# The start of a two-block transformer kernel: order of the first loads, squares summed on TensorE, low parts made between value tiles, constant products ahead of the real ones

## The chip, the cores and the metric

The kernel runs on one core of one Trainium2 chip. The metric is the device time of one execution in microseconds, as the median of several runs. TensorE (PE) does the matrix products, VectorE (DVE) and ScalarE (ACT) work on the elements, GpSimd (POOL) does a power function here, and SyncE (SP) issues most DMAs. ACT and POOL can issue DMAs too.

## What is computed

The reference is a stack of two parts in float32: two layers of a four-branch mixer (differential attention, gated linear attention, latent attention, windowed attention) with a convolutional feed-forward, and then two layers with gated feed-forwards and other mixers. The change touches only the first step of the first layer, which is an RMS norm of 272 tokens (16 meta tokens and 256 inputs) of width 1024, and the product of the normed tokens with the wide matrix `w_in`:

```python
h = jnp.concatenate([meta, x], axis=1)          # 272 tokens x 1024
for l in range(DEPTH):
    u = _rms_norm(h, norm_mix_pre[l])           # x * rsqrt(mean(x*x) + eps) * gain
    (a_q, a_k, a_v, ...) = jnp.split(u @ w_in[l], offsets, axis=-1)
    ...                                         # four branches, gates, w_out
    h = h + _rms_norm(merged @ w_out[l], norm_mix_post[l])
    ...                                         # feed-forward
...                                             # the second block, final norm
```

## The kernel before, in words

The tokens stand transposed in SBUF: `h` holds 8 tiles (k = 0 to 7) of 128 channels by 272 tokens. Every big product is done as three passes in a reduced float32 format: a high part and a low part of both operands, high times high, high times low and low times high (`mm3`). So each weight tile of 128 output columns (8 x 128 values on each partition) is split: `split` writes the high part `wh` on ACT (L114), `split_low` writes the low part `wl` on DVE as the difference (L122). The normed tokens are split in the same way into `uh` and `ul`. Three buffers hold split weight tiles, and three hold raw chunks of 1 MB with two tiles each (`raw`, loaded by `pump_dma`, L100). Products on plain float32 operands run as two instructions each.

Work of each engine runs in the order in which the program writes it; there is no planner behind it. The start goes like this. `setup` issues four token loads (L424, two k each) on SP, then two small loads on ACT, the first three raw chunks on SP, and fourteen small loads on SP (L457: tables, vectors, sinks, constants). Successive DMAs share a limited set of completion semaphores, so an issue can wait for an earlier load to land. `pre` then squares the tokens on ACT as they land (L762), adds the squares of all four pairs on DVE (L764, L766), sums over channels on PE against a column of ones (`tok_sums`, three token blocks), makes mean plus epsilon on DVE (L269), the power -1/2 on POOL (L271), and spreads the three short columns over 128 partitions on PE (`spread`). Ahead of the power in the program, `prefetch(2)` splits the high parts of the first two weight tiles, and behind it `advance` makes their low parts on DVE.

`normed` is the loop that follows: for each k it writes gain times token times spread value (L302, DVE, named `w` in the trace), its high part `uh` (L304, ACT), and, one k later, the low part `ul` (L295, DVE). The first product (`first_gemm` with a group of two weight tiles) goes over k and issues six matmuls for each, three for each of the two tiles; its third and sixth need `wl` of the first and of the second weight tile. Behind the pair come single tiles of 24 matmuls each. The third weight tile's high part is written on ACT behind the last `uh`, its low part on DVE behind the last `ul`.

`gps` and `aps` hand out PSUM buffers in turn, four of each.

Of the kernel before, what the change touches and what calls it, by code (L numbers as in the profile page):

```python
# [13 lines left out]
MUL, ADD, SUB, MAX, MIN = ALU.mult, ALU.add, ALU.subtract, ALU.max, ALU.min  # L14
# [5 lines left out]
KD = 8  # L20
T = 272
META = 16
SEQ = 256
# [11 lines left out]
NR = 3  # L35
# [27 lines left out]
class Kern:  # L63
# [25 lines left out]
        self.phase = -1  # L89
        self.held = False  # L90

    def pump_dma(self):
        while self.n_free < len(self.chunks) and self.chunks[self.n_free].left == 0:
            self.n_free += 1
        while self.n_dma < min(self.n_free + NR, len(self.chunks)):
            c = self.chunks[self.n_dma]
            t = self.wp.tile([128, 2048], F32, tag="raw", name="raw", bufs=NR)
            n = c.nk * c.nc
            src = self.a["weights"][self.offset : self.offset + 128 * n]
            self.nc.sync.dma_start(out=t[:, :n], in_=src.rearrange("(p n) -> p n", p=128))  # L100
            self.offset += 128 * n
            c.tile = t[:, :n].rearrange("p (k c) -> p k c", k=c.nk)
            self.n_dma += 1
# [180 lines left out]
    def w1(self, n=T, bufs=4):  # L284
        return self.wk.tile([128, T], F32, tag="w1", name="w1", bufs=bufs)[:, :n]

    def normed(self, x, pr, gain, shift, n, dst):

        nc = self.nc
        uh, ul = dst  # L290

        def low(k, t):
            h = uh[:, k, :].bitcast(F32)
            if shift is None:
                nc.vector.tensor_tensor(out=ul[:, k, :], in0=t, in1=h, op=SUB)  # L295
            else:
                nc.vector.scalar_tensor_tensor(out=ul[:, k, :], in0=t, scalar=shift(k), in1=h, op0=ADD, op1=SUB)

        prev = None
        for k in range(KD):  # L300
            t = self.w1(n)
            nc.vector.scalar_tensor_tensor(out=t, in0=x[:, k, :], scalar=gain(k), in1=pr, op0=MUL, op1=MUL)  # L302
            if shift is None:
                nc.scalar.activation(uh[:, k, :], t, AF.Copy)  # L304
            else:
                nc.scalar.activation(uh[:, k, :], t, AF.Identity, bias=shift(k))
            if prev is not None:
                low(*prev)
            prev = (k, t)
        low(*prev)  # L310

# [91 lines left out]
    def setup(self):  # L403
        nc, a = self.nc, self.a
        c = self.const
        self.ident = c.tile([128, 128], F32, name="ident")
        self.ones32 = c.tile([128, 32], F32, name="ones32")
        nc.vector.memset(self.ones32, 1.0)
        self.ones = self.ones32[:, 0:1]
        self.zero = c.tile([128, 1], F32, name="zero")  # L410
        nc.vector.memset(self.zero, 0.0)
        self.mhalf = c.tile([128, 16], F32, name="mhalf")
        nc.vector.memset(self.mhalf, -0.5)
        self.shh = c.tile([128, 3], F32, name="shh")


        nc.scalar.activation(self.shh, self.mhalf[:, 0:3], AF.Square)
        self.vec = c.tile([128, sum(n for _, n in VECS)], F32, name="vec")
        self.vecs, o = {}, 0
        for name, n in VECS:  # L420
            self.vecs[name] = o
            o += n
        for k in range(0, KD, 2):
            nc.sync.dma_start(out=self.h[:, k : k + 2, :], in_=a["tokens"][:, k : k + 2, :])  # L424
        n0 = VECS[0][1]
        nc.scalar.dma_start(out=self.ident, in_=a["k_ident"])
        nc.scalar.dma_start(out=self.vec[:, :n0], in_=a["vecs"][:, :n0])
        self.pump_dma()
        self.tabx = self.mx.tile([33, 24], F32, tag="s1", name="tabx", bufs=2)
        nc.vector.memset(self.tabx, NEG)  # L430
        self.hot = self.mx.tile([33, 2, PITCH], F32, tag="s4", name="hot", bufs=3)
        self.dl = self.mx.tile([128, 2, 4, 64], F32, tag="v4", name="dl", bufs=3)
        self.tri = c.tile([128, 2, 128], F32, name="tri")
        self.perm = c.tile([128, 128], F32, name="perm")
        self.cs = c.tile([128, 2, T], F32, name="cs")
        self.lam = c.tile([128, 2], F32, name="lam")
        self.sinks = c.tile([128, 2, 8], F32, name="sinks")
        self.sinkm = c.tile([128, 2, 2], F32, name="sinkm")
        self.mod = c.tile([128, 144], F32, name="mod")
        self.n_mod = 0  # L440
        self.cc = c.tile([128, 8], F32, name="cc")
        s, d = a["swa_sinks"], a["diff_lambda"]
        loads = [
            (self.hot, a["k_hot"]), (self.tabx[0:32, 0:16], a["rel_bias_table"]),
            (self.tabx[0:32, 16:24], a["rel_bias_table"][:, 8:16]), (self.vec[:, n0:], a["vecs"][:, n0:]),
            (self.dl, bass.AP(tensor=d.tensor, offset=d.offset, ap=[[0, 128], [256, 2], [64, 4], [1, 64]])),
            (self.sinks, bass.AP(tensor=s.tensor, offset=s.offset, ap=[[0, 128], [8, 2], [1, 8]])),
        ]
        for h in range(4):
            loads.append((  # L450
                self.sinkm[32 * h : 32 * h + 32],
                bass.AP(tensor=s.tensor, offset=s.offset + h, ap=[[0, 32], [8, 2], [4, 2]]),
            ))
        loads += [(self.cc, a["c_2"].rearrange("a (p k) -> p (a k)", k=8))]
        loads += [(self.tri, a["k_tri"]), (self.perm, a["k_perm"]), (self.cs, a["k_cs"])]
        for dst, src in loads:
            nc.sync.dma_start(out=dst, in_=src)  # L457

    def setup2(self):

# [277 lines left out]
    def mixing(self, l):  # L738
        nc, a = self.nc, self.a
        S = {}  # L740
        r0, rn = (0, T) if l == 0 else (14, T - 14)
        blocks = [BLK["M"], BLK["A"], BLK["B"]]
        W = self.w["w_in"][l]
        x = (self.uh, self.ul)
# [12 lines left out]
        def pre():  # L757
            if l == 0:
                sq = S["merged"]
                acc = sq[:, 0:2, :]  # L760
                for k in range(0, KD, 2):
                    nc.scalar.activation(sq[:, k : k + 2, :], self.h[:, k : k + 2, :], AF.Square)  # L762
                    if k:
                        nc.vector.tensor_tensor(out=acc, in0=acc, in1=sq[:, k : k + 2, :], op=ADD)  # L764
                self.prefetch(2)
                nc.vector.tensor_tensor(out=acc[:, 0, :], in0=acc[:, 0, :], in1=acc[:, 1, :], op=ADD)  # L766
                sums = self.tok_sums([acc[:, 0, :]], blocks)
                r = self.pow_rsqrt(sums, 3, D)
                for j, t in enumerate(sums):
                    nc.vector.tensor_copy(self.shh[:, j : j + 1], t)  # L770
                self.advance()
                pr = self.spread(r, blocks)
                self.normed(self.h, pr[:, :T], lambda k: self.v("norm_mix_pre", l * 8 + k), None, T, x)
            nc.sync.dma_start(out=self.hd[l], in_=self.h)

        self.add(pre)

        def to(name, i, w=128):
# [1642 lines left out]
```

## Time and profile before

| what | us |
|---|---|
| median of 3 runs | 2278.74 |
| lowest and highest of them | 2277.09, 2283.06 |
| the profiled execution's own time | 2284.18 |
| its span, first to last instruction | 2281.6 |
| TensorE busy in it | 2192.9 (96%) |
| VectorE busy | 1612.5 (71%) |
| ScalarE busy | 1217.2 (53%) |

The page gives shares over the whole span. The stage that the change touches is the first 25 us, so it is read from the timeline of each engine there: when an instruction starts, how long it takes, and in brackets how long its engine sat idle before it and who released it. The granted TensorE clock is read from the page's strip and from the views by stretch; ahead of the first record of the clock (at 21.6 us) these views show full speed, and the spacing of the matmuls has to tell the clock there.

### The profile page before, as it was taken

What the parts mean: (1) busy time and instruction counts of PE and PEld (TensorE: products, weight loads), DVE (VectorE), ACT (ScalarE), POOL (GpSimd) and SP (SyncE); (2) the same over time, 40 slices, a digit from 0 to 9 for tenths busy, and PEclk for the clock granted to TensorE, in tenths of its full rate; (3) what the DMA queues carried; (4) which work ended last, traced back from release to release, by engine and by line L of the source; (5) the groups of instructions that cost most, each with busy time, mean ns of one, the idle gap of its engine ahead of it and who ended that gap; (6) DMA issues with size and microseconds to landing.
All of it is one profiled execution on the core that took longest, in us unless ns stands there. A gap on an engine that the chain in (4) does not pass through costs nothing. (4 is left out here: it accounts for less than half of the span.)

```text
span 2281.6 us, 41972 instructions
## 1 busy us (share of the span) xinstructions
PE 2192.9 (96%) x17048; PEld 2070.0 (91%) x17048; DVE 1612.5 (71%) x2809; ACT 1217.2 (53%) x2221; POOL 240.6 (11%) x285
## 2 busy tenths in 40 slices
PE   7999999999999999999999899986999999999998
PEld 7888888899988798788999799986999999989998
DVE  5655454798885555547989887798877787778553
ACT  4555244577556544445775554465644554466442
POOL 0220111100031001112000100066100000001000
PEclk9999999999999999999999899997999999999999
DMA  7553233454764343324657687733687687744551
GB/s 271 190 183 114 100 102 114 172 206 170 278 242 158 112 148 107 112 97 172 227 184 289 260 302 273 255 111 111 229 283 277 241 303 272 268 174 140 206 177 70
DMA packets 73618, 439.21 MB, mean 192 GB/s; under 512 B 14285, under 2 KB 15629, under 8 KB 25936
## 3 DMA queue, kind: packets, MB, share of 16 engines
q1 hardware_dynamic: 62736, 419.66, 51.3%
q0 software_dynamic: 10400, 16.79, 2.5%
q8 instruction: 133, 2.18, 0.4%
q14 instruction: 61, 0.50, 0.1%
q10 hardware_dynamic: 288, 0.07, 0.0%
HBM read 433.12 MB, written 10.01 MB: 194 GB/s over the span
## 5 line engine op out<-in xcount | busy, mean ns | idle before, releaser
L227 PE MATMUL g<-uh,wh 128*128 128x256 f32 (+2 forms) x3560 | 1034.0, 290 | 18.9 <-ACT uh L322 6.2
L227 PE MATMUL g<-ul,wh 128*128 128x256 f32 (+2 forms) x3560 | 1025.1, 288 | 9.5 <-DVE ul L326 5.9
L227 PE MATMUL g<-uh,wl 128*128 128x256 f32 (+2 forms) x3560 | 1021.8, 287 | 2.7 <-DVE wl L122 2.7
L122 DVE TENSOR_TENSOR wl<-raw,wh 128x1024 fp32r<-128x1024 f32 (+2 forms) x660 | 785.8, 1196 | 274.2 <-ACT wh L114 273.7
L114 ACT ACTIVATE wh<-raw 128x1024 fp32r<-128x1024 f32 (+2 forms) x660 | 670.2, 1020 | 335.5 <-PE g L227 298.9
L227 PEld LDWEIGHTS g<-uh,wh 128*128 128x128 f32 x3560 | 680.1, 191 | 42.2 <-issue 13.5
L227 PEld LDWEIGHTS g<-ul,wh 128*128 128x128 f32 x3560 | 678.7, 191 | 14.0 <-DVE ul L326 6.9
L227 PEld LDWEIGHTS g<-uh,wl 128*128 128x128 f32 x3560 | 680.7, 191 | 3.7 <-DVE wl L122 3.4
L227 PE MATMUL g<-gh,wh 128*128 128x256 f32 (+1 forms) x1056 | 299.2, 283 | 0.0
L227 PE MATMUL g<-gh,wl 128*128 128x256 f32 (+1 forms) x1056 | 299.2, 283 | 0.0
L227 PE MATMUL g<-gl,wh 128*128 128x256 f32 (+1 forms) x1056 | 299.1, 283 | 0.0
L227 PEld LDWEIGHTS g<-gl,wh 128*128 128x128 f32 x1056 | 201.5, 191 | 0.0
L227 PEld LDWEIGHTS g<-gh,wh 128*128 128x128 f32 x1056 | 201.3, 191 | 0.0
L227 PEld LDWEIGHTS g<-gh,wl 128*128 128x128 f32 x1056 | 201.3, 191 | 0.0
L1717 DVE CUSTOM_DVE_ANT_0 adaw<-adaw,condb,vec 128x1024 f32<-128x1024 f32 x144 | 182.4, 1280 | 1.5 <-DMA adaw<-in_ada_t_dram 1.5
L1620 DVE SCALAR_TENSOR_TENSOR y<-edge,vec,y 128x272 f32<-128x272 f32 (+1 forms) x176 | 86.4, 493 | 28.5 <-ACT y L1615 25.4
L227 PE MATMUL g<-oh,wh 128*128 128x272 f32 (+1 forms) x296 | 87.9, 297 | 0.0
L227 PE MATMUL g<-ol,wh 128*128 128x272 f32 (+1 forms) x296 | 84.6, 286 | 0.0
L227 PE MATMUL g<-oh,wl 128*128 128x272 f32 (+1 forms) x296 | 84.5, 285 | 0.0
L1863 ACT ACTIVATE sg<-g 128x256 f32<-128x256 f32 x80 | 30.6, 382 | 99.9 <-PE g L227 99.8
L1224 ACT ACTIVATE gt<-g 128x272 f32<-128x272 f32 (+1 forms) x64 | 25.1, 392 | 107.7 <-PE g L227 107.7
L1252 POOL TENSOR_TENSOR merged<-merged,w 128x272 f32<-128x272 f32 (+1 forms) x48 | 37.9, 798 | 338.5 <-DVE w L1251 338.3
(377 smaller groups left out, 2434.2 us busy)
## 6 DMA issues: line engine op xcount, KB each, us to landing
raw<-in_weights_dram SPq DMA_DIRECT2D x294, 1024.0 KB, 4.9
adaw<-in_ada_t_dram SPq DMA_DIRECT2D x72, 1024.0 KB, 6.6
raw<-in_weights_dram SPq DMA_DIRECT2D x28, 768.0 KB, 4.8
skew<-scr POOLq DMA_DIRECT2D x6, 1086.0 KB, 22.7
h<-skew POOLq DMA_DIRECT2D x8, 544.0 KB, 4.4
h<-skew POOLq DMA_DIRECT2D x8, 512.0 KB, 5.4
condb<-cond SPq DMA_DIRECT2D x5, 512.0 KB, 4.7
hd<-h SPq DMA_DIRECT2D x2, 1088.0 KB, 9.1
```

The lines of the kernel that those rows point to most:

```text
L114: self.nc.scalar.activation(h3[:, :, d0 : d0 + n], c.tile[:, :, c0 : c0 + n], AF.Copy)
L122: self.nc.vector.tensor_tensor(out=l3[:, :, d0 : d0 + n], in0=c.tile[:, :, c0 : c0 + n], in1=h3[:, :, d0 : d0 + n].bitcast(F32), op=SUB,)
L227: self.nc.tensor.matmul(out, lhsT, rhs, start=start, stop=stop, skip_group_check=True)
L1224: nc.scalar.activation(t[:, :rn], ps[:, :rn], AF.Tanh, scale=0.5)
L1252: nc.gpsimd.tensor_tensor(out=mg, in0=mg, in1=t, op=ADD)
L1620: nc.vector.scalar_tensor_tensor(out=y, in0=e[:, o : o + on], scalar=cw(i), in1=y, op0=MUL, op1=ADD)
L1717: self.nc.vector.tensor_tensor_reduce(out=t[:, i, :], in0=t[:, i, :], in1=self.condb, scale=1.0, scalar=self.v("ada_b_2", c), op0=MUL, op1 ...
L1863: nc.scalar.activation(t, ps[:, :SEQ], AF.Silu)
```

## The change

In `setup`, the raw chunks are no longer issued, the two small loads on ACT change places, and the fourteen small loads are kept in a list. In `pre`, 14 constant products (`warm`: 32 columns of ones as the stationary operand, 256 columns of ones as the moving one, plain float32) go to PE first. After each square, one raw chunk is issued, on ACT. The small loads follow on SP. DVE adds the squares of the first three pairs only; PE sums two accumulated tiles and the two tiles of the last pair, four for each token block where there was one. Three more constant products follow, then the mean and the power. `prefetch(2)` moves behind them, the `advance` that made the first two low parts goes, and `normed` makes them itself, one each after the low parts of k = 0 and k = 1. One constant product stands between `spread` and the first weight product.

```diff
-    def pump_dma(self):
+    def pump_dma(self, ahead=NR, eng=None):
...
-        while self.n_dma < min(self.n_free + NR, len(self.chunks)):
+        while self.n_dma < min(self.n_free + ahead, len(self.chunks)):
...
-            self.nc.sync.dma_start(out=t[:, :n], in_=src.rearrange("(p n) -> p n", p=128))
+            (eng or self.nc.sync).dma_start(out=t[:, :n], in_=src.rearrange("(p n) -> p n", p=128))
...
-    def normed(self, x, pr, gain, shift, n, dst):
+    def normed(self, x, pr, gain, shift, n, dst, lows=0):
...
             if prev is not None:
                 low(*prev)
+                if k <= lows and self.lows:
+                    self.split_low()
             prev = (k, t)
...
+        nc.scalar.dma_start(out=self.vec[:, :n0], in_=a["vecs"][:, :n0])
         nc.scalar.dma_start(out=self.ident, in_=a["k_ident"])
-        nc.scalar.dma_start(out=self.vec[:, :n0], in_=a["vecs"][:, :n0])
-        self.pump_dma()
...
-        for dst, src in loads:
-            nc.sync.dma_start(out=dst, in_=src)
+        self.loads = loads
+
+    def warm(self, n):
+
+        ps = self.gps()
+        for _ in range(n):
+            self.mm(ps[0:32, :SEQ], self.ones32, self.ones.to_broadcast([128, SEQ]))
...
+                self.warm(14)
                 for k in range(0, KD, 2):
                     nc.scalar.activation(sq[:, k : k + 2, :], self.h[:, k : k + 2, :], AF.Square)
-                    if k:
+
+                    self.pump_dma(k // 2 + 1 if k < KD - 2 else NR, nc.scalar)
+                    if 0 < k < KD - 2:
                         nc.vector.tensor_tensor(out=acc, in0=acc, in1=sq[:, k : k + 2, :], op=ADD)
-                self.prefetch(2)
-                nc.vector.tensor_tensor(out=acc[:, 0, :], in0=acc[:, 0, :], in1=acc[:, 1, :], op=ADD)
-                sums = self.tok_sums([acc[:, 0, :]], blocks)
+                for dst, src in self.loads:
+                    nc.sync.dma_start(out=dst, in_=src)
+                sums = self.tok_sums([sq[:, k, :] for k in (0, 1, 6, 7)], blocks)
+                self.warm(3)
                 r = self.pow_rsqrt(sums, 3, D)
                 for j, t in enumerate(sums):
                     nc.vector.tensor_copy(self.shh[:, j : j + 1], t)
-                self.advance()
+                self.prefetch(2)
                 pr = self.spread(r, blocks)
-                self.normed(self.h, pr[:, :T], lambda k: self.v("norm_mix_pre", l * 8 + k), None, T, x)
+                self.warm(1)
+                self.normed(self.h, pr[:, :T], lambda k: self.v("norm_mix_pre", l * 8 + k), None, T, x, 2)
```

## Rows read from the trace of the kernel before

**Rows 1.** The page, busy time of the bounding engine: us, share, instructions.

```profile
PE 2192.9 (96%) x17048; PEld 2070.0 (91%) x17048; DVE 1612.5 (71%) x2809; ACT 1217.2 (53%) x2221; POOL 240.6 (11%) x285
```

**Rows 2.** Timeline of ACT, first 60 us: start, us, instruction, count, idle and releaser.

```profile
3.59 0.66 ACT L762 ACTIVATE merged<-h 128x544 f32<-128x544 f32 x1 [1.34 <-DMA h<-in_tokens_dram]
...
7.11 1.30 ACT L762 ACTIVATE merged<-h 128x544 f32<-128x544 f32 x2 [1.97 <-DMA h<-in_tokens_dram]
10.24 2.00 ACT L114 ACTIVATE wh<-raw 128x1024 fp32r<-128x1024 f32 x2 [1.83 <-DMA raw<-in_weights_dram]
```

**Rows 3.** Timeline of DVE, first 60 us.

```profile
0.82 0.09 DVE L408 MEMSET ones<- 128x32 f32 x1 [0.82 <-PEq L2411]
...
7.80 1.56 DVE L764 TENSOR_TENSOR merged<-merged 128x544 f32<-128x544 f32 x2 [1.90 <-ACT merged L762]
...
11.63 2.38 DVE L122 TENSOR_TENSOR wl<-raw,wh 128x1024 fp32r<-128x1024 f32 x2
14.30 0.90 DVE L302 SCALAR_TENSOR_TENSOR w<-h,vec,a 128x272 f32<-128x272 f32 x2 [0.30 <-PE a L227]
15.29 0.44 DVE L295 TENSOR_TENSOR ul<-w,uh 128x272 fp32r<-128x272 f32 x1
15.65 0.49 DVE L302 SCALAR_TENSOR_TENSOR w<-h,vec,a 128x272 f32<-128x272 f32 x1
...
17.17 0.49 DVE L302 SCALAR_TENSOR_TENSOR w<-h,vec,a 128x272 f32<-128x272 f32 x1
...
19.86 1.03 DVE L295 TENSOR_TENSOR ul<-w,uh 128x272 fp32r<-128x272 f32 x2
21.39 1.23 DVE L122 TENSOR_TENSOR wl<-raw,wh 128x1024 fp32r<-128x1024 f32 x1 [0.50 <-ACT wh L114]
```

**Rows 4.** Timeline of PE, 9 to 15.5 us: the sums and the spread.

```profile
9.89 1.44 PE L227 MATMUL a<-ones,merged 128*128 128x1 f32 x6 [9.89 <-DVE merged L766]
12.51 1.75 PE L227 MATMUL a<-ident,rs 16*128 16x16 f32 x6 [1.19 <-POOL rs L271]
```

**Rows 5.** Timeline of PE, 15 to 25 us: the pair of weight tiles, then the third tile.

```profile
15.31 0.60 PE L227 MATMUL g<-uh,wh 128*128 128x272 f32 x1 [1.05 <-ACT uh L304]
...
21.40 0.43 PE L227 MATMUL g<-ul,wh 128*128 128x272 f32 x1
21.62 0.36 PE L227 MATMUL g<-uh,wl 128*128 128x272 f32 x1
...
24.33 0.29 PE L227 MATMUL g<-uh,wl 128*128 128x272 f32 x1
24.45 0.28 PE L227 MATMUL g<-uh,wh 128*128 128x272 f32 x1
```

**Rows 6.** The raw tile, instructions up to 12 us: the three first chunks, issue and landing.

```profile
L100 SPq DMA_DIRECT2D raw<-in_weights_dram x3: 427/431/432, 2.6 to 3.6; - x3
...
DMA to landing us min/median/max: 7.6/9.8/12.0
```

**Rows 7.** Timeline of PE elsewhere: plain float32 products, sums and a spread.

```profile
440.97 1.03 PE L227 MATMUL a<-ident,r 16*128 16x16 f32 x6
...
1538.03 2.07 PE L227 MATMUL a<-cy,bd 128*128 128x256 f32 x4 [3.90 <-DVE cy L1957]
...
2271.62 0.61 PE L227 MATMUL a<-ones,acc 128*128 128x1 f32 x4 [0.91 <-DVE acc L1792]
2272.08 0.58 PE L227 MATMUL a<-ones,w 128*128 128x1 f32 x4
```

**Rows 8.** PE by stretches: from:to, length, busy (instructions), granted clock, DMA share, GB/s.

```profile
441.00:444.00 3.00, 1.39 (x8) 1.00 0.02 5
444.00:446.00 2.00, 0.47 (x2) 0.76 0.00 0
446.00:448.00 2.00, 2.00 (x11) 0.50 0.00 0
448.00:450.00 2.00, 2.00 (x16) 0.89 0.00 0
```

## The prediction

> **What bounds the kernel now.** I read the page first. TensorE is busy 96% of the span [rows 1], so a microsecond won or lost ahead of its first weight product is carried to the end, unless a later stall takes it up. The change touches nothing behind the first weight pair, so the stage to read is the first 25 us, engine by engine. On ACT the squares wait for the tokens: the first lands at 3.59, the last two at about 7.1 [rows 2]. On DVE the squares are added, and after the power and the spread the first value tile starts at 14.30 [rows 3]. Call that moment t: the spread is ready and `normed` begins. On PE the six instructions of the sums run from 9.89 to 11.33 and the six of the spread from 12.51 to 14.26 [rows 4]. The first weight product starts at 15.31, 1.01 behind t. From then on matmuls follow each other at 0.22 to 0.23 us until 21.62, afterwards at 0.12; the third weight tile starts at 24.45 [rows 5]. So the pair ran 6.3 us at 1.2 GHz and the rest at 2.4 GHz, and the mark that the change has to move is 24.45, which is t + 10.15. Everything that the change could save lies in these 24.45 us.
>
> **The change part by part.** All times are on the profiled execution (2284.18, span 2281.6, so 2.6 lie outside it). It is 5.4 slower than the median; the runs themselves lie 6 apart. I take the difference at the mark as the difference of the medians.
>
> *Constant products.* They need only the ones, written at 0.82 to 0.91 [rows 3], so PE starts at about 0.95. A plain float32 product is two instructions. Four of them with 256 columns took 2.07 at half clock [rows 7]; less the tail of 0.37 by which a lone matmul (0.60) exceeds the spacing (0.23) [rows 5], that is 0.425 each, and 0.213 at full clock. The 14 products are 28 instructions: 11.9 us if the clock stays at half. The trace shows two rises under continuous work: after 6.3 us [rows 5], and in 446 to 450, where the clock went up at about 448.4 after work that was continuous from 445.5, so after 2.9 [rows 8]. Nothing of before shows how soon it rises from the very start; I take the middle, 4.6, and keep both ends. In 4.6 us 10.8 instructions run, the other 17.2 take 3.7, and the 14 products end at 9.2 (8.4 to 10.05).
>
> *Sums.* PE takes its matmuls in the order written, so the sums stand behind the constant products. If tokens land as before, the squares of the first three pairs are added by 8.58 (half of the two adds from 7.80 [rows 3]) and the last pair's squares are ready by 8.41 [rows 2]; so at 9.2 the sums find both ready, and tokens that land sooner bring nothing. The two adds that go (0.78 and 0.44) went from a wait that is no longer last. In their place PE has 24 instructions instead of six. At full clock four take 0.46 from start to start [rows 7], 0.115 each, so 2.76: sums end at 11.95 (11.15 to 12.8), against 11.33 before.
>
> *Power and spread.* From the end of the sums to the start of the spread it was 1.18 [rows 4]. The three constant products between them take six times 0.213 = 1.28, so the spread starts 1.28 behind. It took 1.75 cold; six such instructions took 1.03 at full clock [rows 7]. With 0.04 to DVE, t = 11.95 + 1.28 + 1.03 + 0.04 = 14.3 (13.5 to 15.15). The clock gives back at the spread what the longer sums cost: t doesn't move (-0.8 to +0.85). The one product behind the spread takes 0.43, inside the 1.01 before the first weight product.
>
> *Low parts inside `normed`.* Before, two low parts took DVE 2.38 from 11.63 [rows 3], hidden under the power and the spread. Now they stand between value tiles, and this cover is gone. In offsets from t: w0 at 0, w1 0.41, low of k = 0 at 0.99, first weight low 1.35, w2 2.54, low of k = 1 2.95, second weight low 3.30 to 4.53, w3 4.49. After that a k takes 0.76 (two in 1.52 [rows 3]): w7 at 7.53, its low part done at 8.97. PE's sixth product needs the second weight low, so only five products run before t + 4.53, and 43 follow. At 2.4 GHz they take 43 times 0.124 = 5.35 and end at t + 9.9; the `ul` are ready in time, just ahead. The third weight tile then waits: its high part is split behind the last `uh` (t + 8.5 to 9.5) and its low part takes 1.23 [rows 3] to t + 10.7, where its third product is due at t + 10.15. The mark becomes t + 10.5, against 10.15: +0.35. Before, that low part was done at 22.62, two microseconds ahead.
>
> *The clock in this gap.* PE has about 1.7 us of work between t and t + 4.53. In 441 to 446 it had 1.86 in 5.0, and the granted clock went to half at about 445.0 for 3.4 us, to 448.4 [rows 8]. If all 3.4 falls on the continuous stretch, 15 products run instead of 27, and 12 times 0.124 = 1.5 are lost: mark t + 11.4, no wait for the low part, +1.3. The stretch of the trace looks alike but PE worked less evenly in it; I take the middle of +0.35 and +1.3, which is +0.8.
>
> *Loads.* The three raw issues (0.43 each [rows 6]) move to ACT, behind the first squares. What stands behind them there are squares that wait for tokens (1.97 idle before the third [rows 2]), so they cost nothing; without that cover, at most 1.3. The first chunk is issued at 3.6 instead of 2.6. Chunks landed 7.6, 9.8 and 12.0 after their issue [rows 6], the first 7.6. I take 7.6, hence 11.2; two high parts (2.00 [rows 2]) end at 13.2, ahead of the first `uh` at t + 0.5 = 14.8. Slack 1.6. The small loads move ahead on SP, and who needs them comes after the mark. The fourth chunk follows the second weight low (t + 4.5) instead of 14.0, but its tiles are due more than 10 us after the mark. The exchange of the two small loads on ACT and the changed turn of the PSUM buffers cost nothing: both loads were done long before.
>
> Sum: 0 + 0.8 = +0.8, from -0.45 (-0.8 + 0.35) to +2.15 (0.85 + 1.3). On the median: 2278.74 + 0.8 = 2279.5.
>
> **The rivals.**
>
> *Early clock.* PE comes to 2.4 GHz sooner and keeps it through the gap. At the limit of full clock from the start, and of tokens so early that the adds are never last, the constant products end at 6.9, the sums at 9.7, and t is 12.0. Then the high parts of the weights are last (13.2), the first product starts at 13.65 instead of 13.0, and the mark is at 12.65 + 10.5 = 23.15: -1.3, 2277.4. For it speaks that the rise was once seen after 2.9; against it, that the half clock at 15.31 lasted 6.3.
>
> *Weights late.* The first chunk is alone on ACT's queue, but the small loads, which stood behind it on SP's queue, are now on another queue beside it. If it lands as late as the third one did, 12.0 after issue [rows 6], it is there at 15.6, the high parts end at 17.6, the first `uh` is written at 18.05 instead of 15.25: +2.8, in all +3.6, 2282.3. Against it speaks that the same bytes moved in the same time before, only in another order. The Trainium skill has a rule that speaks for it: "DMA: Bandwidth & Descriptors", section "Queues, rings and completion order", says that within a queue each DMA engine takes descriptors in order, and that between queues it takes turns. By that rule the weights no longer go ahead of the small loads, and would even share with the last tokens. The landings of before, in order of issue on one queue, agree with its first half; no row shows its second.
>
> *The constant products don't lift the clock.* This is the change not doing what it says, and it ends on the other side. If products of ones leave PE at 1.2 GHz, the 14 end at 12.85; 24 sums at 0.24 (1.44 over six [rows 4]) end at 18.6; three products take 2.55, the spread 1.75, and t is 22.9: +8.6. Of the 43 products 28 run at 0.226 in the 6.3 us before a rise and 15 at 0.124: mark t + 12.7, +2.55 more. In all +11.2, 2289.9. It decides from the point at which the clock is still half when the sums begin. For it speaks that both rises in the rows came under weight products; against it, that these too were matmuls one behind the other, as the 14 are.
>
> **How the numbers follow.** About 0.3% (6.8 us, so 2271.9 to 2285.6) is what a measurement of this kernel can tell from no change. Forecast 0.52, early clock 0.25, weights late 0.15: all within it, 0.92. Constant products without effect 0.05: slower. For faster by 6.8 the stage would have to lose more than a quarter of 24.45, which no row supports; 0.03 for a later stall that happens to vanish. The range 2275.5 to 2283.0 holds the forecast and the first two rivals (2277.4 to 2282.3) with some of the scatter of the runs, and leaves out the third and the tails.
>
> **What would show it.** In the changed profile: PE's first matmul near 0.95, and the spacing of its constant products halving at 4 to 7 us; sums ending near 12.0 and the first value tile near 14.3; two weight lows of 1.2 each between value tiles, with PE idle up to the sixth product; a wait for the third tile's low part, or matmuls at 0.22 behind the gap; the third weight tile at about 25.2 instead of 24.45. The prediction is wrong if that mark moves by more than 3 us, if the clock is at half when the sums begin, or if the time differs while the mark doesn't.

## The result: 11 us slower, and the profile after

The changed kernel's median is 2289.91 us (2286.70 to 2293.46, five runs) beside 2278.47 (2275.22 to 2283.06, five runs) for the kernel before. The ratio is 1.0051, with a 95% interval from 1.0032 to 1.0070: slower, by more than 0.3%. The forecast was 2279.5 with a range up to 2283.0. The profiled execution of the changed kernel took 2292.58, its span 2290.8.

The busy line of the changed kernel's page answers to [rows 1]: PE has 54 instructions more and still about 96% of the span.

```profile
PE 2207.4 (96%) x17102; PEld 2076.8 (91%) x17102; DVE 1611.5 (70%) x2807; ACT 1215.4 (53%) x2221; POOL 240.4 (10%) x285
```

The timeline of ACT in the changed kernel answers to [rows 2] (start, us, instruction, count, idle and releaser; ACTq is ACT's sequencer issuing a DMA).

```profile
3.60 0.38 ACTq L100 DMA_DIRECT2D raw<-in_weights_dram  x1
...
4.36 0.38 ACTq L100 DMA_DIRECT2D raw<-in_weights_dram  x1
6.31 0.66 ACT L771 ACTIVATE merged<-h 128x544 f32<-128x544 f32 x1 [1.30 <-DMA h<-in_tokens_dram]
13.96 0.34 ACTq L100 DMA_DIRECT2D raw<-in_weights_dram  x1
14.35 0.66 ACT L771 ACTIVATE merged<-h 128x544 f32<-128x544 f32 x1 [7.38 <-DMA sinks<-in_swa_sinks_dram]
14.91 1.98 ACT L114 ACTIVATE wh<-raw 128x1024 fp32r<-128x1024 f32 x2
```

The third square ends at 6.97. Then ACT does nothing for 7.38 us: the third chunk of weights is not issued before 13.96, and the fourth square, written behind it, starts at 14.35. Before, that square had run by 8.41. The tile `raw` in the same kernel up to 16 us shows what came at 13.96: the second chunk, issued at 4.36, landed 9.6 later. The view has two landings, of the second chunk (9.6 after its issue) and of the third (9.2); that of the first is not in it.

```profile
L100 ACTq DMA_DIRECT2D raw<-in_weights_dram x3: 335/375/376, 3.6 to 14.0; - x3
...
DMA to landing us min/median/max: 9.2/9.4/9.6
```

The timeline of PE in the changed kernel answers to [rows 4] and [rows 5].

```profile
0.96 9.23 PE L227 MATMUL g<-ones 128*32 128x256 f32 x28 [0.96 <-DVE tabx L433]
10.12 1.50 PE L227 MATMUL a<-ones,merged 128*128 128x1 f32 x12
15.06 2.72 PE L227 MATMUL a<-ones,merged 128*128 128x1 f32 x12 [3.44 <-ACT merged L771]
17.71 2.77 PE L227 MATMUL g<-ones 128*32 128x256 f32 x6
20.40 1.14 PE L227 MATMUL a<-ident,rs 16*128 16x16 f32 x6
21.47 0.62 PE L227 MATMUL g<-ones 128*32 128x256 f32 x2
22.60 0.39 PE L227 MATMUL g<-uh,wh 128*128 128x272 f32 x1 [0.50 <-ACT uh L306]
...
26.10 0.60 PE L227 MATMUL g<-uh,wl 128*128 128x272 f32 x1 [0.85 <-DVE wl L122]
...
33.75 0.29 PE L227 MATMUL g<-uh,wh 128*128 128x272 f32 x1
```

The first twelve sum instructions take 1.50 (0.125 each, full clock). The other twelve need the last square, wait, and take 2.72 (0.227, half clock). The third weight tile, the mark of the prediction, starts at 33.75 instead of 24.45 [rows 5]: 9.3 later in these two profiles. A second profile of each gave 34.27 and 22.27, so 12.0. The medians differ by 11.4. From the mark to the end of the span the two kernels take the same, 2257.0 (changed) and 2257.2 in the first profiles, 2252.7 and 2252.0 in the second, so the loss is ahead of the mark.

DVE in the changed kernel answers to [rows 3]: the first value tile (t) is at 21.58 instead of 14.30.

```profile
21.58 0.91 DVE L304 SCALAR_TENSOR_TENSOR w<-h,vec,a 128x272 f32<-128x272 f32 x2 [3.41 <-PE a L227]
...
22.93 1.22 DVE L122 TENSOR_TENSOR wl<-raw,wh 128x1024 fp32r<-128x1024 f32 x1
24.07 0.49 DVE L304 SCALAR_TENSOR_TENSOR w<-h,vec,a 128x272 f32<-128x272 f32 x1
...
24.83 1.22 DVE L122 TENSOR_TENSOR wl<-raw,wh 128x1024 fp32r<-128x1024 f32 x1
25.97 0.49 DVE L304 SCALAR_TENSOR_TENSOR w<-h,vec,a 128x272 f32<-128x272 f32 x1
```

The view by stretches of the changed kernel (from:to, length, busy of PE, PEld, DVE, ACT, POOL, granted clock, DMA share, GB/s) shows the clock. It falls while PE waits for the last square, and again between the value tiles.

```profile
13.00:14.00 1.00, 0.00 (x0) 0.00 (x0) 0.00 (x0) 0.00 (x0) 0.00 (x0) 0.92 0.37 101
14.00:16.00 2.00, 0.94 (x5) 0.94 (x5) 0.00 (x0) 1.65 (x3) 0.00 (x0) 0.50 0.05 2
16.00:20.00 4.00, 4.00 (x15) 2.58 (x14) 0.67 (x6) 0.89 (x1) 0.85 (x1) 0.50 0.34 125
...
24.00:26.00 2.00, 1.04 (x3) 0.72 (x3) 2.00 (x5) 0.43 (x1) 0.00 (x0) 0.52 0.00 0
26.00:30.00 4.00, 3.90 (x17) 3.90 (x18) 3.85 (x12) 2.19 (x6) 0.00 (x0) 0.50 0.70 176
```

### The profile page after: what moved, and what is told of

The parts are those of the page before. It is cut to its first block, busy times and chain, and to the rows that moved or that the text cites. A ratio compares the mean times of both kernels' runs of the same rounds, so it can differ in the third digit from the quotient of the medians.

```text
span 2290.8 us, 42076 instructions
## 1 busy us (share of the span) xinstructions
PE 2207.4 (96%) x17102; PEld 2076.8 (91%) x17102; DVE 1611.5 (70%) x2807; ACT 1215.4 (53%) x2221; POOL 240.4 (10%) x285
## 5 line engine op out<-in xcount | busy, mean ns | idle before, releaser
L227 PEld LDWEIGHTS g<-ul,wh 128*128 128x128 f32 x3560 | 678.6, 191 | 13.8 <-DVE ul L330 6.9
```

Source lines behind the costliest of these rows:

```text
L227: self.nc.tensor.matmul(out, lhsT, rhs, start=start, stop=stop, skip_group_check=True)
```

## The experiments

What was in question: whether the held issue is the whole loss, and if not, which other part costs the rest. Four parts can be taken singly: the order of the loads, the sums on PE, the low parts between value tiles, and the constant products. All kernels compute the whole result. The table has all runs. "Square" is the start of the fourth square, "sums" the end of the sums, t the first value tile, "mark" the third weight tile, "later" the 145th weight product, which is the first of the seventh tile; by then what the clock lost or won around the pair is counted in. Ratios are to runs of the kernel before on the same chip (median 2278.47 for the changed kernel, 2276.90 to 2277.34 for the others); they come from all runs and are not the quotients of the medians.

| kernel | median | ratio [95%] | square | sums | t | mark | later |
|---|---|---|---|---|---|---|---|
| before (first profile) | 2278.47 | | 7.75 | 11.33 | 14.30 | 24.45 | 38.77 |
| before again | 2276.04 (one run) | | 7.17 | 10.56 | 13.54 | 22.27 | 36.59 |
| changed | 2289.91 | 1.0051 [1.0032, 1.0070] | 14.35 | 17.77 | 21.58 | 33.75 | 48.08 |
| changed again | 2288.75 (one run) | | 14.89 | 18.32 | 22.74 | 34.27 | 48.60 |
| third chunk on SP | 2284.03 | 1.0022 [1.0006, 1.0039] | 7.26 | 12.73 | 16.50 | 29.19 | 43.51 |
| small loads later | 2284.62 | 1.0025 [1.0014, 1.0035] | 6.77 | 12.96 | 16.51 | 27.88 | 42.20 |
| no products | 2288.79 | 1.0048 [1.0026, 1.0069] | 14.32 | 17.75 | 20.73 | 33.49 | 47.81 |
| load order alone | 2287.19 | 1.0042 [1.0021, 1.0062] | 14.24 | 17.62 | 20.61 | 29.60 | 43.92 |
| all but load order | 2285.05 | 1.0020 [1.0003, 1.0038] | 6.26 | 11.97 | 16.40 | 28.13 | 42.45 |
| the same, sums on DVE | 2281.17 | 1.0012 [0.9996, 1.0027] | 7.19 | 10.66 | 13.08 | 25.72 | 40.04 |
| all but load order, products between sums | 2288.09 | 1.0038 [1.0025, 1.0050] | 8.07 | 13.49 | 15.90 | 27.44 | 41.76 |
| products alone | 2276.66 | 0.9995 [0.9981, 1.0009] | 7.30 | 10.08 | 13.17 | 20.71 | 35.72 |
| low parts alone | 2281.47 | 1.0015 [1.0002, 1.0027] | 7.47 | 10.85 | 13.83 | 25.15 | 39.47 |
| sums alone | 2279.61 | 1.0013 [0.9995, 1.0031] | 7.19 | 12.90 | 15.88 | 25.48 | 39.80 |

**Third chunk on SP.** The changed kernel, with the third raw chunk issued on SP behind the small loads.

```diff
-                    self.pump_dma(k // 2 + 1 if k < KD - 2 else NR, nc.scalar)
+                    self.pump_dma(min(k // 2 + 1, 2), nc.scalar)
...
+                self.pump_dma()
```

> The changed kernel with one edit: the third raw chunk is issued by SP behind the small loads instead of by ACT ahead of the fourth square. Theory A (ACT is held ahead of the fourth square, because the issue of the third chunk waits for the semaphore of the second chunk's landing): the fourth square starts at 6.5 to 7.5 instead of 14.35, the sums end at 11.5 to 13, the spread is ready (first value tile) at 14 to 15.5, the third weight tile starts at 24.5 to 26.5, and the time is 2278 to 2281. Theory B (the constant products, the longer sums on PE and the low parts between value tiles are what costs, and ACT's wait is hidden behind them): the third weight tile stays at 31 to 34 and the time at 2286 to 2290.

The fourth square is back at 7.26. In the timeline of ACT:

```profile
7.26 0.66 ACT L771 ACTIVATE merged<-h 128x544 f32<-128x544 f32 x1 [0.33 <-DMA h<-in_tokens_dram]
10.69 2.00 ACT L114 ACTIVATE wh<-raw 128x1024 fp32r<-128x1024 f32 x2 [2.78 <-DMA raw<-in_weights_dram]
```

It waits for its tokens alone, and the later tile comes 4.57 sooner than in the changed kernel. The held issue is a cause, and about half of the loss (4.57 of 9.31 at the later tile; the ratio falls from 1.0051 to 1.0022), but t is 16.50, not the forecast 14.3, and the mark is 29.19: something else is lost too.

**No products.** The changed kernel without its 18 constant products.

```diff
-                self.warm(14)
...
-                self.warm(3)
...
-                self.warm(1)
```

> The changed kernel without its 18 constant products. Theory A: the fourth square still starts at about 14.3; only the three products behind the sums are won, and the clock is at half as before; third weight tile at 31 to 34, time 2286 to 2290. Theory B: with the products gone the sums end by 12, third weight tile at 25.5 or earlier, time 2277 to 2281.

The hold is the same (square at 14.32) and so, nearly, is the mark. The products in the changed kernel neither cause the loss nor win anything: what they lift is lost while PE waits for the last square.

**Load order alone.** The kernel before, with the change's order of loads (the two small loads on ACT exchanged too) and nothing else of it.

```diff
...
-        self.pump_dma()
...
-        for dst, src in loads:
-            nc.sync.dma_start(out=dst, in_=src)
+        self.loads = loads
...
+                    self.pump_dma(k // 2 + 1 if k < KD - 2 else NR, nc.scalar)
...
+                for dst, src in self.loads:
+                    nc.sync.dma_start(out=dst, in_=src)
```

> The kernel before with the order of the loads alone: raw chunks on ACT behind the squares, small loads behind them on SP, the two small loads on ACT exchanged; no products, all squares added on DVE, low parts as before. Theory A: the fourth square starts at about 14 instead of 7.75, all behind it moves by about 6.5, third weight tile at 30 to 32 instead of 24.45, time 2284 to 2287. Theory B: third weight tile at 24 to 25.5, time 2277 to 2280.

The timeline of ACT has the same hold:

```profile
13.86 0.33 ACTq L100 DMA_DIRECT2D raw<-in_weights_dram  x1
14.24 0.66 ACT L760 ACTIVATE merged<-h 128x544 f32<-128x544 f32 x1 [7.43 <-DMA sinks<-in_swa_sinks_dram]
```

With none of the other parts the time rises by 0.42%, the largest of the four parts taken singly.

**All but load order.** The changed kernel with the loads as before: the three chunks and the small loads back in `setup`, all on SP.

```diff
...
+        self.pump_dma()
...
-        self.loads = loads
+        for dst, src in loads:
+            nc.sync.dma_start(out=dst, in_=src)
...
-                    self.pump_dma(k // 2 + 1 if k < KD - 2 else NR, nc.scalar)
...
-                for dst, src in self.loads:
-                    nc.sync.dma_start(out=dst, in_=src)
```

> The changed kernel with the loads in the order of before (raw chunks on SP in the setup, small loads behind them); products, sums on PE and low parts between value tiles as in the change. Theory A: the fourth square at about 7.75, the sums end at 12 to 13, first value tile at 14 to 15.5, third weight tile at 24.5 to 26.5, time 2278 to 2281. Theory B: third weight tile at 31 to 34, time 2286 to 2290.

The fourth square runs at 6.26, sooner than in any other run, although the weights stand right behind the tokens on SP. In the eight profiles with that order it starts at 6.26 to 8.07, in the two with the change's order and no hold at 6.77 and 7.26: no gain shows from asking for the weights later. Still the kernel is slower than before, so the other three parts together cost time. The timeline of PE shows where it begins, and the view of PE by stretches (granted clock behind the busy time) why:

```profile
8.79 3.19 PE L227 MATMUL a<-ones,merged 128*128 128x1 f32 x24
11.90 2.77 PE L227 MATMUL g<-ones 128*32 128x256 f32 x6
14.60 1.76 PE L227 MATMUL a<-ident,rs 16*128 16x16 f32 x6
```

```profile
10.00:11.00 1.00, 1.00 (x11) 1.00 1.05 442
11.00:12.00 1.00, 1.00 (x7) 0.56 0.97 410
```

The clock falls at 11.1, inside the row of 24 sum instructions, though PE never paused. So the three products and the spread run at 1.2 GHz.

**The same, sums on DVE.** All but load order, with the last adds back on DVE and six sum instructions.

```diff
-                    if 0 < k < KD - 2:
+                    if k:
...
-                sums = self.tok_sums([sq[:, k, :] for k in (0, 1, 6, 7)], blocks)
+                nc.vector.tensor_tensor(out=acc[:, 0, :], in0=acc[:, 0, :], in1=acc[:, 1, :], op=ADD)
+                sums = self.tok_sums([acc[:, 0, :]], blocks)
```

> All of the change but the order of the loads and the sums: products and low parts between value tiles as in the change, squares added on DVE, six sum instructions. Theory C: against the run with all but the load order (sums end 11.97, value tiles from 16.40, third weight tile 28.13) the products behind the sums and the spread run at full clock, value tiles start at 13 to 14, third weight tile at 23.5 to 25.5. Theory D: value tiles from 15.5 or later, third weight tile at 27 to 28.5.

Timeline of PE:

```profile
9.83 0.83 PE L227 MATMUL a<-ones,merged 128*128 128x1 f32 x6
10.59 1.49 PE L227 MATMUL g<-ones 128*32 128x256 f32 x6
12.01 1.03 PE L227 MATMUL a<-ident,rs 16*128 16x16 f32 x6
```

The products take 1.49 instead of 2.77, the spread 1.03 instead of 1.76, and t is 3.3 sooner. But the mark is only 2.4 sooner, since the clock that is kept to t is lost behind it (by stretches, the same columns):

```profile
16.00:17.00 1.00, 0.35 (x3) 0.83 0.37 96
17.00:18.00 1.00, 0.40 (x2) 0.50 0.05 0
```

**Products between sums.** All but load order, with one constant product behind each of the first three groups of six sum instructions.

```diff
-    def tok_sums(self, sqs, blocks):
+    def tok_sums(self, sqs, blocks, between=False):
...
+            if between and i < len(sqs) - 1:
+                self.warm(1)
...
-                sums = self.tok_sums([sq[:, k, :] for k in (0, 1, 6, 7)], blocks)
+                sums = self.tok_sums([sq[:, k, :] for k in (0, 1, 6, 7)], blocks, True)
```

> As the run with all of the change but the order of the loads (sums on PE, 24 instructions; there the clock fell at 11.1 and value tiles started at 16.40), with one more constant product behind each of the first three groups of six sum instructions. Theory C (the clock falls because a row of sum instructions doesn't hold it): the clock stays at full through the sums and the spread in spite of 1.3 us more work; spread of about 1.03, value tiles from 14.7 to 15.5. If the clock falls for the time since its rise or for another reason: products behind the sums and the spread at half clock, value tiles from 17 or later.

Timeline of PE:

```profile
12.66 0.83 PE L227 MATMUL a<-ones,merged 128*128 128x1 f32 x6
13.41 1.49 PE L227 MATMUL g<-ones 128*32 128x256 f32 x6
14.84 1.03 PE L227 MATMUL a<-ident,rs 16*128 16x16 f32 x6
```

The same 24 sum instructions, and the clock stays at 2.4 GHz: from the sums to t it takes 2.41 instead of 4.43. So the uninterrupted row of sums is what lost the clock. The mark is 0.7 sooner than in all but load order; the median isn't lower. Its profile has the clock at half from 277 to 291 us, behind everything that the edit touches. Such a stretch also comes without the edit: the first profile of the kernel before has such a stretch from 274 to 288, the first of the changed kernel from 283 to 297, the second profile of each has none. Here is a part of it, this kernel first, then the first profile of before (PE by stretches):

```profile
280.00:285.00 5.00, 5.00 (x29) 0.50 0.00 0
```

```profile
280.00:285.00 5.00, 5.00 (x30) 0.50 0.00 0
```

From the later tile to the end of the span this kernel takes 2245.1, all but load order 2237.6, the kernel before 2242.8 with such a stretch and 2237.7 without. So that stretch, not the start, puts this profile behind. Why all seven runs of this kernel are above 2286, and whether the edit makes the stretch more frequent, stays open.

**Products alone.** The kernel before with the 18 products and nothing else: `warm` as in the change, 14 ahead of the squares, three ahead of the power, one behind the spread.

```diff
+                self.warm(14)
...
+                self.warm(3)
...
+                self.warm(1)
```

> The kernel before with the constant products alone (14, 3, 1): loads, squares added on DVE, six sum instructions and low parts ahead of the spread as before. Theory C (the clock, once at full, is lost behind the row of 24 sum instructions, so the products behind the sums, the spread and half of the first weight products run at half clock): with six sum instructions the clock stays up; sums end at 10 to 11, spread ready at 13 to 13.5, first value tile at 14.0 (behind the low parts), third weight tile at 21.5 to 23 instead of 24.45, time 1 to 3 below the kernel before. Theory D (constant products never carry the clock over sums and spread): products at half clock behind the sums, third weight tile at 24.5 or later, time the same or above.

Timeline of PE:

```profile
9.25 0.83 PE L227 MATMUL a<-ones,merged 128*128 128x1 f32 x6
...
11.43 1.03 PE L227 MATMUL a<-ident,rs 16*128 16x16 f32 x6
...
20.71 0.29 PE L227 MATMUL g<-uh,wh 128*128 128x272 f32 x1
...
21.54 0.40 PE L227 MATMUL g<-uh,wl 128*128 128x272 f32 x1 [0.41 <-DVE wl L122]
```

The pair runs at full clock and the mark comes at 20.71, against 24.45 and 22.27 in the two profiles of before. The third tile's low part is then late by 0.41, and at the later tile 3.05 or 0.87 is left. In the medians that is 0.9995 [0.9981, 1.0009]: not distinguishable from before, and some 12 us under the changed kernel in its second run. No other variant was as low.

**Low parts alone.** The kernel before, without `advance` ahead of the spread's use and with the two low parts inside `normed`.

```diff
-    def normed(self, x, pr, gain, shift, n, dst):
+    def normed(self, x, pr, gain, shift, n, dst, lows=0):
...
+                if k <= lows and self.lows:
+                    self.split_low()
...
-                self.advance()
...
-                self.normed(self.h, pr[:, :T], lambda k: self.v("norm_mix_pre", l * 8 + k), None, T, x)
+                self.normed(self.h, pr[:, :T], lambda k: self.v("norm_mix_pre", l * 8 + k), None, T, x, 2)
```

> The kernel before with one edit: the low parts of the first two weight tiles between the value tiles, not ahead of the spread. First value tile at 14.3 as before, PE's sixth product at 18.8, the other 43 at half clock until a rise 3 to 6 us later: third weight tile at 25.5 to 27.5, time 1 to 3 above. Were the low parts free there, the third weight tile would stay at 24.45.

The sixth product (timeline of PE) waits for its low part, and the mark is 11.32 behind t instead of 10.15 or 8.73:

```profile
18.34 0.60 PE L227 MATMUL g<-uh,wl 128*128 128x272 f32 x1 [0.85 <-DVE wl L122]
```

The part costs time by itself: 1.0015 [1.0002, 1.0027].

**Sums alone.** The kernel before with the adds of the last pair and of the two accumulated tiles moved to PE.

```diff
-                    if k:
+                    if 0 < k < KD - 2:
...
-                sums = self.tok_sums([acc[:, 0, :]], blocks)
+                sums = self.tok_sums([sq[:, k, :] for k in (0, 1, 6, 7)], blocks)
```

> The kernel before with one edit: four tiles summed on PE (24 instructions at half clock, about 0.23 each) instead of one behind two more adds on DVE. Sums end at 13.8 to 14.5 instead of 11.3, spread ready at 16.8 to 17.5, third weight tile at 26.5 to 28, time 2 to 4 above. Were the sums on PE as short as the adds that they replace, the third weight tile would stay at 24.45.

Timeline of PE:

```profile
7.62 5.28 PE L227 MATMUL a<-ones,merged 128*128 128x1 f32 x24 [7.62 <-DVE merged L764]
```

At half clock the row takes 5.28 and t comes 1.6 to 2.3 later; in the medians 1.0013 [0.9995, 1.0031], unclear by itself.

**Small loads later.** The changed kernel with the fourteen small loads issued on SP just ahead of the store at the end of `pre`. The third chunk stays on ACT.

```diff
-                for dst, src in self.loads:
-                    nc.sync.dma_start(out=dst, in_=src)
...
+            if l == 0:
+                for dst, src in self.loads:
+                    nc.sync.dma_start(out=dst, in_=src)
```

> The changed kernel with one edit: the small loads are issued on SP behind the fourth raw chunk, so that the third raw chunk is the ninth DMA and shares a semaphore with the first token load; it is still issued by ACT ahead of the fourth square. Theory A (the hold is the shared semaphore, not the issue on ACT): the fourth square at 6.5 to 7.7, sums end at 11.5 to 13, value tiles from 15 to 17, third weight tile at 27.5 to 29.5, time 2281 to 2285. If the issue on ACT itself were what holds the square (a full queue behind two chunks of 1 MB), the fourth square stays at 13 to 15 and the third weight tile at 32 to 34.

The timeline of ACT:

```profile
6.09 0.66 ACT L771 ACTIVATE merged<-h 128x544 f32<-128x544 f32 x1 [1.12 <-DMA h<-in_tokens_dram]
6.09 0.33 ACTq L100 DMA_DIRECT2D raw<-in_weights_dram  x1
6.77 0.66 ACT L771 ACTIVATE merged<-h 128x544 f32<-128x544 f32 x1
```

The same issue, on the same engine, at the same place in the program, now goes out at 6.09. So it isn't the issuing on ACT that costs; it is which DMAs stand ahead of it in the whole program. In the changed kernel as built, eight completion semaphores are handed to the DMAs in turn. The third chunk is the 20th DMA and gets the semaphore of the 12th, the second chunk; with the small loads later it is the ninth, and has the semaphore of the first token load, which lands by 3.6. The numbering is read from the built programs, and the traces record the same semaphores for these issues; the runs vary it only in this way.

**Before again, and changed again.** Both kernels unchanged, one profiled execution each.

> The kernel before, unchanged, for the scatter of its start: the third weight tile between 22 and 25 (24.45 in the first profile), first value tile between 13.5 and 14.5.

> The changed kernel, unchanged, for the scatter of its start: the fourth square held again until the second chunk has landed (13 to 15), the third weight tile between 32 and 35 (33.75 in its first profile).

The hold repeats (square at 14.89). The start of the kernel before varies by 2.2 us at the mark between two profiles: its last tokens land sooner and its clock rises at 17.7 instead of 21.6. Differences of a microsecond or two at the mark of single profiles are therefore not read as effects.

The expected places in time were missed in several runs. All but load order fits neither theory (t at 16.40 and the mark at 28.13, where 14 to 15.5 and 24.5 to 26.5, or a mark of 31 to 34, were expected), and third chunk on SP has the same miss behind the sums. Products between sums has t at 15.90 instead of 14.7 to 15.5, sums alone ends its sums at 12.90 instead of 13.8 to 14.5, and products alone is 0.5 below the kernel before (2277.16 on that chip) instead of 1 to 3.

## Why the prediction was wrong, step by step

From the changed kernel to the one before, at the later tile: undoing the hold gives 4.57, the rest of the load order 1.06, the sums back on DVE 2.41, the low parts back (with `prefetch(2)` where it was) 4.32, and taking the products away costs 3.05. Together 9.31, which is 48.08 less 38.77. These are single profiles in one order of undoing, so the 1.06 is not shown to be an effect; against the second profile of before, the last step is 0.87. The share of each hangs on what else is in the kernel: low parts alone cost 0.7 to 2.9 there, where PE is at half clock until 21.3 in any case, so there is less clock to lose.

**Loads: the step that failed.** "What stands behind them there are squares that wait for tokens ..., so they cost nothing; without that cover, at most 1.3." It counted an issue as its 0.43 us and left out what an issue waits for. The first two behaved as said (3.60, 4.36). The third waited 7 us for the second chunk's semaphore, with the fourth square behind it. The text ahead of the prediction says that an issue can wait for an earlier load to land; the prediction didn't ask for each moved issue which load that is. Its price was in reach: a second chunk issued at about 4.3 that lands 7.6 to 9.8 later [rows 6] holds the square until 11.9 to 14.1, against its start at 7.75 before. (That view has two landings too, 7.6 of the first chunk and 12.0 of the third; 9.8 is their middle and not, as the prediction reads it, a landing.)

The releaser that the profile names, `sinks`, misleads: that load comes later on the semaphore of the fourth token load, which the square also waits for, and the tokens had long landed (7.17 to 7.75 is when the square runs where nothing holds it in the kernel before).

**Constant products: right in what they do, a little short in time.** They started at 0.96 and ended at 10.19 (forecast 9.2, outer bound 10.05), in other runs at 8.8 to 10.2. In the changed kernel their spacing halves behind the one at 6.94, 6.0 after the start where 4.6 was taken; in the other runs with products the clock rose 3.2 to 6.1 after it. The clock was full when the sums began. The third rival, that the products don't lift the clock, is thereby refuted; that its 2289.9 is the measured number is a coincidence.

**Sums: right in length, wrong in what they leave.** 24 in 2.84 with the third chunk on SP, forecast 2.76. But the clock falls during the row or just behind it.

**Power and spread: mis-sized through that clock.** Forecast 1.28 and 1.03. With the third chunk on SP 2.05 and 1.76, in the changed kernel 2.69 and 1.14. That (0.8 and 0.7 more with the third chunk on SP), with first products that end 0.75 later, is why t is 16.50 and not 14.3 even without the hold.

**Low parts inside `normed`: placed right to 0.1.** In the changed kernel, offsets from t: first weight low 1.35 (1.35 forecast), w2 2.49 (2.54), second weight low 3.25 (3.30), w3 4.39 (4.49), sixth product 4.52 (4.53).

**The clock in this gap: mis-sized.** The mark was forecast at t + 10.5 to 11.4. In the changed kernel it is at 12.17 and 11.53, in the other runs with these low parts at 11.3 to 12.8. The bound was "if all 3.4 falls on the continuous stretch"; in the changed kernel the clock stayed at half from 24.1 to 30.8, and 4.7 of that fell on the continuous stretch, which begins at 26.10. That is 21 products at 0.226 where 38 fit at 0.124, so 2.1 lost instead of 1.5. The 3.4 of [rows 8] was the shorter of the two cases at hand; [rows 5] has 6.3. The comparison with 10.15 also hid a price: that is a pair at half clock. With the products alone the pair keeps its clock and the mark is at t + 7.54, so with these low parts the changed kernel is 4.0 to 4.6 behind that.

**Rivals.** Early clock needed early tokens and a kept clock; neither helped, as the sums lose it. Weights late did not come true: the first chunk, which holds both tiles of the pair, was there 7.0 after its issue with the third chunk on SP (3.65, and 10.69 in ACT's line there), not 12.0, and in the changed kernel its high parts (14.91 to 16.89) were held by ACT alone and ended before t. The 9.6 of the second chunk mattered only through the issue that waited for it. The prediction's own signs were clear: the mark moved by over 3 us, and the time with it.

## What to carry to other kernels

Before a DMA issue is moved to a compute engine's queue, or ahead of other DMAs, find for it which earlier DMA its semaphore comes from and when that lands; all work behind it on that engine starts no earlier. Constant products lift the clock, but the gain is kept only if the work behind them keeps it too, so a row of small sums or a stretch of waits between them and the real products gives it away. Work moved out of a stretch where it hid under another wait, such as these low parts under the power, costs its length and the clock that PE loses meanwhile.

## What the runs showed of the hardware

- **A row of sums lost the clock without a pause.** In all but load order, 24 sum instructions ran in a row, at 0.11 each from start to start, and the granted clock fell from 1.00 to 0.50 at 11.1 us, 2.3 us into the row; with a constant product behind each of the first three groups of six it stayed at 1.00.
- **Weights land later beside small loads on another queue.** The first chunk, issued at 3.6 in both, landed 7.0 us after its issue with the third chunk on SP, and 5.6 with the small loads later. There, the tile `raw` has the landings of the first and the third chunk:

```profile
DMA to landing us min/median/max: 5.6/6.8/8.1
```

The Trainium skill, "DMA: Bandwidth & Descriptors", section "Queues, rings and completion order", says that a DMA engine takes turns between the queues it has work for. The changed kernel's trace agrees with it, the half for which no row of before spoke: from 10 to 12 us, with the second chunk (issued at 4.36) still on its way, ACT's queue q10 and SP's queue q1 with the small loads issued from 6.30 on moved data side by side (the DMA view of that stretch: packets, MB, share of the 16 engines).

```profile
q10 hardware_dynamic: 74, 0.57, 68.9%
q1 hardware_dynamic: 82, 0.25, 31.5%
```
